# Two weight-block orders and two sign conventions for a seven-product block multiplication in a decoder layer

## The chip, the cores and the metric

The kernel runs on one core of a Trainium2 chip. The core has five engines with queues of their own: TensorE (PE in the profile; its weight loads are listed as PEld), VectorE (DVE), ScalarE (ACT), GpSimd (POOL) and SyncE (SP, which here only issues transfers). Each engine executes its queue in order and waits at semaphores for the others. The metric is the device time of one execution in microseconds (us); the median of three executions of the kernel before is 1702.04 us (1701.92 to 1702.26).

## What is computed

One decoder layer on 256 tokens of width 2048: a feed-forward block, a token mixer, a second feed-forward block, each with a residual sum, and a final norm.

```python
def swiglu(h, w_in, w_out):
    gu = h @ w_in                                # 2048 x 11264
    gate, up = gu[..., :D_FF], gu[..., D_FF:]
    return (jax.nn.silu(gate) * up) @ w_out      # 5632 x 2048

h = h + 0.5 * swiglu(rmsnorm(h, ffn1_norm[l]), ffn1_w_in[l], ffn1_w_out[l])
u = rmsnorm(h, mix_norm[l]) @ w_in_mix[l]
...
h = h + jnp.concatenate([y_pool, y_gla], axis=-1) @ w_out_mix[l]
h = h + 0.5 * swiglu(rmsnorm(h, ffn2_norm[l]), ffn2_w_in[l], ffn2_w_out[l])
return rmsnorm(h, final_norm)
```

All is float32. The change touches only the two `swiglu` blocks (and the way their weights are laid out), which take most of the time.

## The kernel before

**Precision.** A float32 product is made of three matmuls of a shorter type (`fp32r`): each operand is split into a high part (a rounding cast on ACT, line 155) and a low part (the source minus the high part, on DVE, line 156), and `three` (line 188) adds high x high, high x low and low x high. So each 128x512 block of weights costs ACT a cast and DVE a subtraction before PE can use it, and each product of a 128-token tile with a block costs PE three matmuls of 128x512.

**Steps.** Weights are streamed once, in steps of four blocks (1 MB): two 128-row blocks of the contraction by two 512-column blocks, B11 B12 / B21 B22. Activations of the same step are 2x2 blocks as well (two tiles of 128 tokens). There are two kinds of step:

- An S step (`s_step`, line 167, `Group.s`) is the plain 2x2 block product: 8 products, 24 matmuls. It splits the four blocks as they are: one 128x2048 subtraction on DVE where the buffers allow it.
- A W step (`w_step`, line 173, `Group.w`, line 260) is Winograd's form with 7 products, 21 matmuls. It needs sums of weight blocks (T1 to T4, made by `less`, line 179, on DVE, in place over the loaded blocks) and sums of activation blocks (S1 to S4, made once per pair of activation blocks by `s_factors`). It splits seven blocks: B11, B22, B21, then T1, T3, T2, T4. Three of the loaded blocks are therefore split before they are overwritten. Products shared between outputs are kept in two PSUM tiles of their own (`pw_...`), which `combine` (line 288) adds up when the last W step of a group is done (one ACT copy, four DVE operations of 128x512, then two of 128x1024 at line 483).

**Loops.** `ffn` (line 435) goes over 11 chunks of 512 gate and 512 up columns. `first_product(c)` takes 8 steps over the 2048 rows; which are W is given by `KINDS` (line 62): none in the first chunks, 4 or 5 of 8 in the next, then `CHUNKS`, 6 of 8 in each of the eight late chunks. The W steps come first in a chunk, over the activation pairs `W_PAIRS`; then the S steps. At the chunk's end come silu and product (lines 490 and 492), transposes on PE (line 499, output `ftp` or `ztp`) and a split (line 505). Between the chunks `second_product` takes S steps alone: 4 for each chunk. The output tiles on PE are named `ps_fi`, `pw_fi` (first product), `ps_fo` (second product) in the first feed-forward block and `ps_zi`, `pw_zi`, `ps_zo` in the second.

**Buffers.** Loaded steps go to a ring of raw buffers (`ring_raw`, 3, and one more per feed-forward block, `fring_raw` or `zring_raw`). Split blocks go to a ring of block buffers, high and low: 16 in `ring_hi`, `ring_lo`, and `MORE_RING` = 6 more in `fring_` or `zring_`, so 22. Blocks are taken in turn; a run of blocks that crosses the end of one part of the ring is split into two operations (`parts_of`, line 145). A block's buffer is free again when PE has done its last matmul with it.

**What sets the order.** The code is written step by step; the framework's scheduler, which uses a timeline model of its own, then sets each engine's queue, interleaving steps. The queues are fixed when the kernel is built.

Of the kernel before, what the change touches and what calls it, by code (L numbers as in the profile page):

```python
# [33 lines left out]
ALU = mybir.AluOpType  # L34
PSUM = bass.MemoryType.PSUM

P = 128
# [5 lines left out]
CW = 512  # L43
# [13 lines left out]
REACH = 16  # L57


W_PAIRS = (1, 3, 4, 6, 2, 5)  # L60
CHUNKS = ("WWWWWWSS",) * 8
KINDS = {
    "f": ("SSSSSSSS", "SSSSSSSS", "WWSWWWSS") + CHUNKS,
    "z": ("SSSSSSSS", "SWSWWWSS", "WWSWWWSS") + CHUNKS,
# [7 lines left out]
RAW_BUFS = 3  # L72
RING = 16
MORE_RAW = 1
MORE_RING = 6
WIDE = True
ROW_AT = 7
S_AT = 3
# [4 lines left out]
def layer(ctx: ExitStack, tc: tile.TileContext, io):  # L83
    nc = tc.nc
# [60 lines left out]
    def parts_of(src, runs, cw=CW):  # L145

        res = []
        for x in runs:
            i = x.start
            while i < x.stop:  # L150
                n, new = blocks.take(x.stop - i)
                hi, lo = (y[:, :, :cw] for y in new)
                for j in range(0, n, 2):
                    k = min(j + 2, n)
                    nc.scalar.copy(out=hi[:, j:k, :], in_=src[:, i + j : i + k, :])  # L155
                nc.vector.tensor_tensor(  # L156
                    out=lo, in0=src[:, i : i + n, :], in1=hi.bitcast(F32), op=ALU.subtract
                )
                res += [(hi[:, j, :], lo[:, j, :]) for j in range(n)]
                i += n  # L160
        return res

    ALL, PAIRS = (slice(0, 4),), (slice(0, 2), slice(2, 4))
# [3 lines left out]
    def s_step(src, parts=1, runs=WIDE):  # L167

        w = load(src, parts=max(parts, 2)).rearrange("p (b c) -> p b c", c=CW)
        b = parts_of(w, SINGLES if parts == 4 else PAIRS if parts == 2 or not WIDE else ALL)  # L170
        return lambda k, n: b[n if k == 0 else 3 - n]

    def w_step(src):

        w = load(src).rearrange("p (b c) -> p b c", c=CW)
        f = dict(zip(("B11", "B22", "B21"), parts_of(w, (slice(0, 1), slice(2, 4)))))

        def less(out, x, y):
            nc.vector.tensor_tensor(out=out, in0=x, in1=y, op=ALU.subtract)  # L179


        less(w[:, 0:2, :], w[:, 1:2, :].broadcast_to([P, 2, CW]), w[:, 0:4:2, :])
        less(w[:, 2, :], w[:, 2, :], w[:, 0, :])
        less(w[:, 3, :], w[:, 3, :], w[:, 2, :])
        f.update(zip(("T1", "T3", "T2", "T4"), parts_of(w, PAIRS)))
        return f

    def three(ps, a, b, start, stop, **kw):

        for i, (x, y) in enumerate(((a[0], b[0]), (a[0], b[1]), (a[1], b[0]))):  # L190
            nc.tensor.matmul(ps, x, y, start=start and i == 0, stop=stop and i == 2, **kw)  # L191

    class Group:
# [66 lines left out]
        def w(self, a, s, b):  # L260

            if self.one is None:
                self.one = [
                    self.psum[self.tags[1]].tile(
                        [P, 2, CW], F32, tag=self.tags[1], name=f"pw_{self.name}_{i}"
                    )
                    for i in range(2)
                ]
                first = True
            else:  # L270
                first = False
            self.left_w -= 1
            last = self.left_w == 0
            p16, p75 = self.one
            for (t, n), x, y in (((0, 0), a(0, 1), b["B21"]), ((0, 1), s["S4"], b["B22"])):
                ps, start, stop = self.target(t, n)
                three(ps, x, y, start, stop)
            three(p16[:, 0, :], a(0, 0), b["B11"], first, last)
            three(p75[:, 1, :], s["S1"], b["T1"], first, last)
            three(p75[:, 0, :], s["S3"], b["T3"], first, last)  # L280
            three(p16[:, 1, :], s["S2"], b["T2"], first, last)
            ps, start, stop = self.target(1, 0)
            three(ps, a(1, 1), b["T4"], start, stop)
            self.n += 1
            if last:
                self.combine()

        def combine(self):

            p16, p75 = self.one  # L290
            self.add = [
                ftmp[0].tile([P, 2, CW], F32, tag=f"add{t}", name=f"add_{self.name}_{t}")
                for t in range(NT)
            ]
            c, d = self.add
            u2 = d[:, 1, :]
            nc.scalar.copy(out=c[:, 0, :], in_=p16[:, 0, :])
            nc.vector.tensor_tensor(out=u2, in0=p16[:, 1, :], in1=c[:, 0, :], op=ALU.add)
            nc.vector.tensor_tensor(out=c[:, 1, :], in0=p75[:, 1, :], in1=u2, op=ALU.add)
            nc.vector.tensor_tensor(out=d[:, 0, :], in0=p75[:, 0, :], in1=u2, op=ALU.add)  # L300
            nc.vector.tensor_tensor(out=d[:, 1, :], in0=p75[:, 1, :], in1=d[:, 0, :], op=ALU.add)

# [345 lines left out]
    def finish1(np_, grp, h):  # L650
# [22 lines left out]
        finish1, first=x_ahead,  # L673
# [31 lines left out]
    for t in range(NT):  # L705
# [6 lines left out]
            out=gsil[t][:, gw[0] + gw[1] :], in_=ps[t][:, : gw[2]], func=AF.Silu, scale=rs(t)  # L712
# [13 lines left out]
    for t in range(NT):  # L726
        nc.vector.scalar_tensor_tensor(
            out=la[:, t, :], in0=z[t], scalar=0.0, in1=e[:, t, :], op0=ALU.min, op1=ALU.subtract
# [63 lines left out]
    for t in range(NT):  # L792
        sp = ps_t.tile([P, HEADS, P], F32, tag="tp", name=f"sp{t}")
        c = slice(t * P, (t + 1) * P)
# [339 lines left out]
```

## Time and profile before

| | |
|---|---|
| median of three executions | 1702.04 us |
| the profiled execution, span from first to last instruction | 1702.4 us |
| TensorE clock granted, mean | 0.998 |
| instructions on PE and on DVE in the profile | 7705 and 1565 |
| HBM read, written | 338.75 MB, 25.17 MB |
| stretches: first feed-forward block, mixer and its output product, second feed-forward block | about 0 to 700, 700 to 1000, 1000 to 1700 us |

In the profile a busy matmul overlaps the next one (matmuls are pipelined), so PE's busy share says little about how much of its rate is used; the distance between the starts of matmuls does. DVE's operations overlap at their ends too, by some 0.08 us. The span of the profiled execution stands 0.4 us above the median, so differences worked out in it can be taken from the median as they are.

### The profile page before, as it was taken

Reading aid. Unit: us, or ns where it says so; the run is one execution under the profiler, and the core shown is the slowest. Engines: PE = TensorE matmul, PEld = TensorE weight load, DVE = VectorE, ACT = ScalarE, POOL = GpSimd, SP = SyncE. Lnnn points to the kernel's source line nnn. Section 1 sums busy time; section 2 is a strip of 40 time slices with the busy share of each in tenths; the row PEclk is TensorE's granted clock in tenths of the full one; section 3 lists DMA queues with packets and bytes.
Section 4 is the critical chain, followed back from the end, with each engine's and each line's share of the span. In section 5 each row is a group of like instructions: output and inputs, shape, how many; then the busy total and the mean of one; then the engine's idle time right before and its main releaser. Section 6 shows DMA issues by size and latency. Waiting matters only on the chain.

```text
span 1702.4 us, 20984 instructions
## 1 busy us (share of the span) xinstructions
PE 1689.7 (99%) x7705; PEld 1403.1 (82%) x7705; DVE 1411.5 (83%) x1565; ACT 999.3 (59%) x1272; POOL 62.9 (4%) x70
## 2 busy tenths in 40 slices
PE   9999999999999999999999999999999999999997
PEld 7888888888888888888988888888888888888886
DVE  8779999999999996645564677999999999998974
ACT  7655666665666664563454554666656656566553
POOL 0000000000000000000000000000000000000012
PEclk9999999999999999999999999999999999999999
DMA  9856856857767776554665764676666667677781
GB/s 355 338 142 229 259 156 229 269 165 221 259 178 221 246 240 215 185 182 139 197 214 169 228 203 155 196 249 195 214 244 208 203 235 227 192 245 218 215 298 50
DMA packets 105241, 365.30 MB, mean 215 GB/s; under 512 B 11809, under 2 KB 15009, under 8 KB 105138
## 3 DMA queue, kind: packets, MB, share of 16 engines
q1 hardware_dynamic: 97026, 335.63, 58.1%
q0 software_dynamic: 7392, 27.27, 8.1%
q8 instruction: 60, 0.98, 0.2%
q10 hardware_dynamic: 720, 1.07, 0.2%
q14 instruction: 43, 0.35, 0.1%
HBM read 338.75 MB, written 25.17 MB: 214 GB/s over the span
## 4 chain that ended last, share of the span: by engine, by line
PE 91%; DVE 5%; DMA 2%; issue 1%; ACT 1%; SPq 0%; POOL 0%; POOLq 0%; ACTq 0%; DVEq 0%
PE ps_fi L191 17%; PE ps_zi L191 14%; PE ps_fo L191 14%; PE ps_zo L191 12%; PE pw_fi L191 8%; PE pw_zi L191 7%; PE ps_h L191 5%; PE ps_mp L191 3%; PE ps_mv L191 3%; DVE ring_lo L156 2%; PE ps_mg L191 2%; PE ps_mq L191 1%; DMA ring_raw<-in_ffn_w_out 1%; PE ps_w_mk L191 1%; DVE ring_raw L179 1%
## 5 line engine op out<-in xcount | busy, mean ns | idle before, releaser
L155 ACT CAST ring_hi<-ring_raw 128x1024 fp32r<-128x1024 f32 (+3 forms) x544 | 501.4, 942 | 381.6 <-DMA ring_raw<-in_ffn_w_in 79.8
L156 DVE TENSOR_TENSOR ring_lo<-ring_raw,ring_hi 128x1024 fp32r<-128x1024 f32 (+6 forms) x463 | 573.8, 1250 | 182.5 <-ACT ring_hi L155 181.4
L179 DVE TENSOR_TENSOR ring_raw<-ring_raw 128x512 f32<-128x512 f32 (+1 forms) x243 | 207.4, 862 | 0.3
L155 ACT CAST zring_hi<-ring_raw 128x1024 fp32r<-128x1024 f32 (+1 forms) x113 | 99.6, 887 | 54.5 <-DMA ring_raw<-in_ffn_w_out 11.8
L191 PE MATMUL ps_fi<-ring_lo,xT_hi 128*128 128x512 f32 x324 | 126.5, 390 | 0.5 <-DVE ring_lo L156 0.4
L191 PE MATMUL ps_fi<-ring_hi,xT_lo 128*128 128x512 f32 x324 | 125.8, 389 | 0.0
L191 PE MATMUL ps_fi<-ring_hi,xT_hi 128*128 128x512 f32 x324 | 124.2, 390 | 1.2 <-ACT ring_hi L155 1.2
L156 DVE TENSOR_TENSOR zring_lo<-ring_raw,zring_hi 128x1024 fp32r<-128x1024 f32 (+3 forms) x101 | 112.2, 1117 | 11.9 <-ACT zring_hi L155 11.8
L155 ACT CAST ring_hi<-zring_raw 128x1024 fp32r<-128x1024 f32 (+1 forms) x85 | 84.2, 991 | 48.0 <-PE ps_zi L191 22.8
L191 PE MATMUL ps_zi<-ring_lo,h_hi 128*128 128x512 f32 x288 | 112.1, 389 | 0.0
L191 PE MATMUL ps_zi<-ring_hi,h_lo 128*128 128x512 f32 x288 | 112.1, 390 | 0.0
L191 PE MATMUL ps_zi<-ring_hi,h_hi 128*128 128x512 f32 x288 | 111.3, 390 | 0.0
L156 DVE TENSOR_TENSOR ring_lo<-zring_raw,ring_hi 128x1024 fp32r<-128x1024 f32 (+2 forms) x65 | 94.2, 1451 | 7.4 <-ACT ring_hi L155 7.3
L191 PE MATMUL ps_fo<-ring_lo,fhi 128*128 128x512 f32 x240 | 93.9, 391 | 0.0
L191 PE MATMUL ps_fo<-ring_hi,flo 128*128 128x512 f32 x240 | 93.8, 391 | 0.0
L191 PE MATMUL ps_fo<-ring_hi,fhi 128*128 128x512 f32 x240 | 93.4, 391 | 0.0
L191 PE MATMUL pw_zi<-ring_hi,s_z 128*128 128x512 f32 x262 | 92.5, 389 | 0.0
L191 PE MATMUL ps_zo<-ring_lo,zhi 128*128 128x512 f32 x234 | 91.5, 391 | 0.0
L191 PE MATMUL ps_zo<-ring_hi,zlo 128*128 128x512 f32 x234 | 91.4, 391 | 0.0
L191 PE MATMUL ps_zo<-ring_hi,zhi 128*128 128x512 f32 x234 | 90.7, 390 | 0.0
L191 PE MATMUL pw_fi<-ring_hi,s_f 128*128 128x512 f32 x226 | 78.7, 389 | 0.0
L155 ACT CAST ring_hi<-fring_raw 128x512 fp32r<-128x512 f32 (+1 forms) x69 | 56.9, 832 | 33.6 <-DVE fring_raw L179 9.8
(324 smaller groups left out, 3730.5 us busy)
## 6 DMA issues: line engine op xcount, KB each, us to landing
ring_raw<-in_ffn_w_in SPq DMA_DIRECT2D x262, 512.0 KB, 5.6
ring_raw<-in_ffn_w_out SPq DMA_DIRECT2D x136, 512.0 KB, 5.2
fring_raw<-in_ffn_w_in SPq DMA_DIRECT2D x44, 512.0 KB, 5.5
zring_raw<-in_ffn_w_in SPq DMA_DIRECT2D x44, 512.0 KB, 4.3
ring_raw<-in_w_out_mix SPq DMA_DIRECT2D x32, 512.0 KB, 4.3
fring_raw<-in_ffn_w_out SPq DMA_DIRECT2D x20, 512.0 KB, 6.0
zring_raw<-in_ffn_w_out SPq DMA_DIRECT2D x20, 512.0 KB, 6.0
hd<-half_f POOLq DMA_DIRECT2D x18, 512.0 KB, 8.1
```

The costliest lines, as they stand in the source:

```text
L155: nc.scalar.copy(out=hi[:, j:k, :], in_=src[:, i + j : i + k, :])
L156: nc.vector.tensor_tensor(out=lo, in0=src[:, i : i + n, :], in1=hi.bitcast(F32), op=ALU.subtract)
L179: nc.vector.tensor_tensor(out=out, in0=x, in1=y, op=ALU.subtract)
L191: nc.tensor.matmul(ps, x, y, start=start and i == 0, stop=stop and i == 2, **kw)
```

## The change

It does five things.

1. The four blocks of a step are laid out B12, B11, B22, B21 in HBM instead of B11, B12, B22, B21 (`steps`, line 1083), and `s_step` picks them accordingly.
2. In `w_step` the three blocks that are needed as they are (B11, B22, B21) now lie side by side and are split in one call, and the four sums are split in another. The sums are made with other signs: Q1 = B11 + B12 in place of T1 = B12 - B11, with the whole second column of blocks turned in sign inside the form. There is an addition of 128x512 (line 181 of the kernel after), a subtraction of 128x512 and one of two blocks at once (line 179).
3. `combine` takes two differences instead of two sums.
4. `CHUNKS`: of the eight late chunks, the first, third, fifth and seventh have 7 W steps of 8; the others keep 6. Per feed-forward block that is four S steps that become W steps. `W_PAIRS` gets a seventh pair, 0, whose activation sums S1 to S4 have to be made and kept in each feed-forward block.
5. `MORE_RING` goes from 6 to 5: the block ring has 21 buffers.

```diff
--- before.py
+++ after.py
@@ -57,8 +57,8 @@
 REACH = 16
 
 
-W_PAIRS = (1, 3, 4, 6, 2, 5)
-CHUNKS = ("WWWWWWSS",) * 8
+W_PAIRS = (1, 3, 4, 6, 2, 5, 0)
+CHUNKS = ("WWWWWWWS", "WWWWWWSS") * 4
 KINDS = {
     "f": ("SSSSSSSS", "SSSSSSSS", "WWSWWWSS") + CHUNKS,
     "z": ("SSSSSSSS", "SWSWWWSS", "WWSWWWSS") + CHUNKS,
@@ -72,7 +72,7 @@
 RAW_BUFS = 3
 RING = 16
 MORE_RAW = 1
-MORE_RING = 6
+MORE_RING = 5
 WIDE = True
 ROW_AT = 7
 S_AT = 3
@@ -168,21 +168,20 @@
 
         w = load(src, parts=max(parts, 2)).rearrange("p (b c) -> p b c", c=CW)
         b = parts_of(w, SINGLES if parts == 4 else PAIRS if parts == 2 or not WIDE else ALL)
-        return lambda k, n: b[n if k == 0 else 3 - n]
+        return lambda k, n: b[1 - n if k == 0 else 3 - n]
 
     def w_step(src):
 
         w = load(src).rearrange("p (b c) -> p b c", c=CW)
-        f = dict(zip(("B11", "B22", "B21"), parts_of(w, (slice(0, 1), slice(2, 4)))))
+        f = dict(zip(("B11", "B22", "B21"), parts_of(w, (slice(1, 4),))))
 
         def less(out, x, y):
             nc.vector.tensor_tensor(out=out, in0=x, in1=y, op=ALU.subtract)
 
-
-        less(w[:, 0:2, :], w[:, 1:2, :].broadcast_to([P, 2, CW]), w[:, 0:4:2, :])
-        less(w[:, 2, :], w[:, 2, :], w[:, 0, :])
-        less(w[:, 3, :], w[:, 3, :], w[:, 2, :])
-        f.update(zip(("T1", "T3", "T2", "T4"), parts_of(w, PAIRS)))
+        nc.vector.tensor_tensor(out=w[:, 0, :], in0=w[:, 0, :], in1=w[:, 1, :], op=ALU.add)
+        less(w[:, 2, :], w[:, 0, :], w[:, 2, :])
+        less(w[:, 1:4:2, :], w[:, 1:4:2, :], w[:, 2:3, :].broadcast_to([P, 2, CW]))
+        f.update(zip(("Q1", "T3", "T2", "T4"), parts_of(w, ALL)))
         return f
 
     def three(ps, a, b, start, stop, **kw):
@@ -276,7 +275,7 @@
                 ps, start, stop = self.target(t, n)
                 three(ps, x, y, start, stop)
             three(p16[:, 0, :], a(0, 0), b["B11"], first, last)
-            three(p75[:, 1, :], s["S1"], b["T1"], first, last)
+            three(p75[:, 1, :], s["S1"], b["Q1"], first, last)
             three(p75[:, 0, :], s["S3"], b["T3"], first, last)
             three(p16[:, 1, :], s["S2"], b["T2"], first, last)
             ps, start, stop = self.target(1, 0)
@@ -296,9 +295,9 @@
             u2 = d[:, 1, :]
             nc.scalar.copy(out=c[:, 0, :], in_=p16[:, 0, :])
             nc.vector.tensor_tensor(out=u2, in0=p16[:, 1, :], in1=c[:, 0, :], op=ALU.add)
-            nc.vector.tensor_tensor(out=c[:, 1, :], in0=p75[:, 1, :], in1=u2, op=ALU.add)
+            nc.vector.tensor_tensor(out=c[:, 1, :], in0=p75[:, 1, :], in1=u2, op=ALU.subtract)
             nc.vector.tensor_tensor(out=d[:, 0, :], in0=p75[:, 0, :], in1=u2, op=ALU.add)
-            nc.vector.tensor_tensor(out=d[:, 1, :], in0=p75[:, 1, :], in1=d[:, 0, :], op=ALU.add)
+            nc.vector.tensor_tensor(out=d[:, 1, :], in0=p75[:, 1, :], in1=d[:, 0, :], op=ALU.subtract)
 
 
 
@@ -1080,7 +1079,7 @@
 
         b = np.stack([left, right], 2).reshape(-1, 2, P, left.shape[1], 2, CW)
         b = b.transpose(3, 0, 2, 1, 4, 5)
-        b = np.stack([b[:, :, :, 0, 0], b[:, :, :, 0, 1], b[:, :, :, 1, 1], b[:, :, :, 1, 0]], 3)
+        b = np.stack([b[:, :, :, 0, 1], b[:, :, :, 0, 0], b[:, :, :, 1, 1], b[:, :, :, 1, 0]], 3)
         return b.reshape(b.shape[0], b.shape[1], P, 4 * CW)
 
     def quads(w):
```

Built, the PE queue has 24 matmuls of 128x512 fewer (6942 in place of 6966), all from the eight changed steps; the DVE queue has 152 instructions fewer (1415 in place of 1567), and no transfer is added or taken away. Two places show how rows moved.

The first is the start of the program on PE, the first S step of the first chunk, whose four blocks are loaded and split one by one. `ps_fi_0` and `ps_fi_1` are the outputs of the two token tiles, `ring_hi` and `ring_lo` the parts of a weight block, `xT_hi` and `xT_lo` those of the activations; in brackets stands the engine whose semaphore is waited for. Before:

```order
L191 MATMUL ps_fi_0_137<-ring_hi,xT_hi_114 128x512 [waits Activation_49]
L191 MATMUL ps_fi_0_137<-ring_lo,xT_hi_114 128x512 [waits DVE_49]
L191 MATMUL ps_fi_0_137<-ring_hi,xT_lo_118 128x512
L191 MATMUL ps_fi_0_137<-ring_hi,xT_hi_114 128x512 [waits Activation_49]
L191 MATMUL ps_fi_0_137<-ring_lo,xT_hi_114 128x512 [waits DVE_49]
L191 MATMUL ps_fi_0_137<-ring_hi,xT_lo_118 128x512
L191 MATMUL ps_fi_0_137<-ring_hi,xT_hi_114 128x512 [waits Activation_49]
L191 MATMUL ps_fi_1_138<-ring_hi,xT_hi_114 128x512 [waits PE_49]
```

and after the change:

```order
L190 MATMUL ps_fi_0_137<-ring_hi,xT_hi_114 128x512 [waits Activation_49]
L190 MATMUL ps_fi_0_137<-ring_lo,xT_hi_114 128x512 [waits DVE_49]
L190 MATMUL ps_fi_0_137<-ring_hi,xT_lo_118 128x512
L190 MATMUL ps_fi_0_137<-ring_hi,xT_hi_114 128x512
L190 MATMUL ps_fi_0_137<-ring_lo,xT_hi_114 128x512
L190 MATMUL ps_fi_0_137<-ring_hi,xT_lo_118 128x512
L190 MATMUL ps_fi_0_137<-ring_hi,xT_hi_114 128x512 [waits Activation_49]
L190 MATMUL ps_fi_1_138<-ring_hi,xT_hi_114 128x512 [waits PE_49]
```

The first product now uses the second block to be loaded instead of the first, so the second product (fourth row) no longer waits for a cast; the seventh row, the first that uses the second row of blocks, waits for ACT in both.

The second place is DVE in the first feed-forward block, where the sums of the fourth chunk have been combined and the W steps of the fifth are being prepared. Rows with `fring_raw` as their source all belong to one W step; the others belong to the steps around it or to the chunk that has ended (`flo`). Before, from that step's first split to its last:

```order
L156 TENSOR_TENSOR ring_lo<-fring_raw,ring_hi 128x512
L156 TENSOR_TENSOR ring_lo<-fring_raw,ring_hi 128x1024
L179 TENSOR_TENSOR fring_raw<-fring_raw 128x1024
L179 TENSOR_TENSOR fring_raw<-fring_raw 128x512
L505 TENSOR_TENSOR flo_1587<-ftp_1577,fhi_1586 128x4x128
L179 TENSOR_TENSOR fring_raw<-fring_raw 128x512
L156 TENSOR_TENSOR ring_lo<-fring_raw,ring_hi 128x1024
L156 TENSOR_TENSOR fring_lo<-ring_raw,fring_hi 128x512
L156 TENSOR_TENSOR ring_lo<-fring_raw,ring_hi 128x512
L505 TENSOR_TENSOR flo_1587<-ftp_1577,fhi_1586 128x4x128
L156 TENSOR_TENSOR fring_lo<-fring_raw,fring_hi 128x512
```

and after the change, for the W step in the same place (its addition at line 181 stands some ten rows earlier, in between the chunk's sums):

```order
L156 TENSOR_TENSOR ring_lo<-fring_raw,ring_hi 128x1536
L179 TENSOR_TENSOR fring_raw<-fring_raw 128x512
L504 TENSOR_TENSOR flo_1579<-ftp_1569,fhi_1578 128x4x128
L181 TENSOR_TENSOR ring_raw<-ring_raw 128x512
L179 TENSOR_TENSOR fring_raw<-fring_raw 128x2x512
L156 TENSOR_TENSOR ring_lo<-ring_raw,ring_hi 128x1536
L504 TENSOR_TENSOR flo_1579<-ftp_1569,fhi_1578 128x4x128
L179 TENSOR_TENSOR ring_raw<-ring_raw 128x512
L156 TENSOR_TENSOR ring_lo<-fring_raw,ring_hi 128x2048
```

Eight operations have become five: the splits of one and two blocks are one of three blocks, the last three splits are one of four blocks (2048 columns), and the three operations on sums remain three. The last split, on which all four products with sums now wait, comes after the operation on two blocks and not before it in part.

## The prediction

> **What bounds the kernel now.** I read the page first, then PE's waits, then the distances between matmuls, then DVE by stretches. The page's busy times, two of its 40-slice rows and the chain that ended last:
>
> ```profile
> PE 1689.7 (99%) x7705; PEld 1403.1 (82%) x7705; DVE 1411.5 (83%) x1565; ACT 999.3 (59%) x1272; POOL 62.9 (4%) x70
> PE   9999999999999999999999999999999999999997
> DVE  8779999999999996645564677999999999998974
> ...
> PE 91%; DVE 5%; DMA 2%; issue 1%; ACT 1%; SPq 0%; POOL 0%; POOLq 0%; ACTq 0%; DVEq 0%
> ```
>
> PE is never idle, the chain runs over PE for 91%, but in both feed-forward blocks DVE has nines as well. So two engines are near their limits there. PE's own waits, all that the view of waits has for PE:
>
> ```profile
> PE idle L575 <- DVE zeros L570: 1.2, 1, 1.2
> PE ps_fi L191 <- ACT ring_hi L155: 1.2, 2, 0.8
> PE ps_fi L191 <- DVE ring_lo L156: 0.4, 2, 0.2
> ```
>
> That is under 3 us in 1702. Busy matmuls overlap, so I check that PE runs at its rate by their starts; this is the first and the last of 24 that follow each other in the second block (PE's timeline):
>
> ```profile
> 1195.66 0.39 PE L191 MATMUL ps_zi<-ring_hi,h_hi 128*128 128x512 f32 x1
> ...
> 1200.87 0.39 PE L191 MATMUL ps_zi<-ring_lo,h_hi 128*128 128x512 f32 x1
> ```
>
> 23 distances in 5.21 us are 0.2265 us each, which is what a matmul costs here (its "0.39" is mostly overlap). An S step's 24 take 5.44 us, a W step's 21 take 4.76 us. So PE, fed without a gap, sets the time, and a matmul taken away is worth 0.2265 us as long as DVE keeps feeding it. How near DVE is, over three late chunks of the second block (busy us and number of instructions by engine):
>
> ```profile
> 1161.00:1224.00 63.00, 63.00 (x284) 52.26 (x283) 58.60 (x61) 39.01 (x46) 2.23 (x3) 1.00 0.67 209
> 1224.00:1286.00 62.00, 62.00 (x279) 51.33 (x278) 59.44 (x62) 38.68 (x46) 1.71 (x2) 1.00 0.69 221
> 1286.00:1348.00 62.00, 62.00 (x279) 51.36 (x278) 57.75 (x61) 37.88 (x45) 1.71 (x2) 1.00 0.70 221
> sum 187.00, PE 187.00 PEld 154.95 DVE 175.79 ACT 115.57 POOL 5.66; mean PE 62.33 PEld 51.65 DVE 58.60 ACT 38.52 POOL 1.89
> ```
>
> DVE works 58.6 us of a chunk's 62.33, so 3.7 us are left. Where they lie decides much. The same view for a stretch in which DVE prepares W steps and one in which it prepares S steps:
>
> ```profile
> 1138.00:1184.00 46.00, 46.00 (x208) 38.08 (x207) 45.10 (x50) 28.03 (x34) 1.70 (x2) 1.00 0.61 177
> 1184.00:1196.00 12.00, 12.00 (x55) 9.94 (x54) 8.26 (x7) 7.55 (x9) 0.00 (x0) 1.00 0.95 331
> ```
>
> For W steps DVE is busy 98%; its rest is in the S steps (69%). There it waits for ACT, and ACT for buffers that PE still uses, or for a load:
>
> ```profile
> 1185.65 1.05 ACT L155 CAST ring_hi<-zring_raw 128x1024 fp32r<-128x1024 f32 x1 [3.47 <-PE ps_zi L191]
> ...
> 1191.60 1.05 ACT L155 CAST ring_hi<-ring_raw 128x1024 fp32r<-128x1024 f32 x1 [1.57 <-DMA ring_raw<-in_ffn_w_out]
> ```
>
> So this idle time is mostly DVE being ahead with a full ring: W steps use up a lead, S steps build it up again.
>
> **The change, part by part.**
>
> *Matmuls.* Eight S steps become W steps: 8 x 3 = 24 matmuls fewer, 24 x 0.2265 = **-5.4 us**, all on the path.
>
> *DVE's cost of a step.* What an operation costs is the distance to the next one that doesn't wait. Four rows without a wait between them:
>
> ```profile
> 1196.02 2.28 DVE L156 TENSOR_TENSOR ring_lo<-ring_raw,ring_hi 128x2048 fp32r<-128x2048 f32 x1
> 1198.22 0.68 DVE L298 TENSOR_TENSOR add_zi<-pw_zi,add_zi 128x512 f32<-128x512 f32 x1
> 1198.83 1.22 DVE L156 TENSOR_TENSOR zring_lo<-ring_raw,zring_hi 128x1024 fp32r<-128x1024 f32 x1
> 1199.96 0.68 DVE L299 TENSOR_TENSOR add_zi<-pw_zi,add_zi 128x512 f32<-128x512 f32 x1
> ```
>
> 512 columns cost 0.61, 1024 cost 1.13, 2048 cost 2.20; 1536 lie between, 1.67. A W step without cuts at the ring's ends is now 3 x 0.61 + 4 x 1.13 = 6.35 us and becomes 1.67 + 2 x 0.61 + 1.13 + 2.20 = 6.22; an S step stays at 2.20. Joining two operations saves only about 0.07 us. The Trainium skill (VectorE: DVE Perf Modes, The DRAIN you can't avoid) says that a next operation doesn't start before the pipe has emptied; then whole durations would count, a step's two operations fewer would be worth about 0.3 us, and the change would be nearly free for DVE. The starts above contradict it by 0.06 to 0.09 us an operation, so I keep the distances.
>
> A late chunk with 7 W steps: one more W step has 3.5 x 1024 more columns, each worth 2.20 - 1.13 = 1.07, so +3.75 us. 152 instructions fewer over 22 chunks are 7 a chunk, 7 x 0.07 = -0.5 us. DVE then needs 58.6 + 3.75 - 0.5 = 61.85 us, and PE 62.33 - 3 x 0.2265 = 61.65. A chunk with 6: 58.1 against 62.33. A pair: **119.95 of DVE in 123.98 of PE**. The spare shrinks from 7.5 to 4.0 us a pair, but stays positive, so on average DVE feeds PE.
>
> *The lead.* What counts is the worst moment, the end of a run of W steps. Four things shorten the lead there: the seventh W step uses up 6.22 - 4.76 = 1.46; the ring has one block fewer, a seventh of a W step, 0.68; all sums wait for one split of 2.20 where they waited for one of 1.13, 1.07; and DVE gains back 0.5. Together 2.7 us. How much is there now? A place where one value is written once and read once is the transpose at the chunk's end. The second `za` is written from 1145.74 on, and PE reads it at 1151.21:
>
> ```profile
> 1145.74 0.75 DVE L492 SCALAR_TENSOR_TENSOR za<-ps_zi,r_h_r,zs 128x512 f32<-128x512 f32 x1
> ...
> 1151.21 0.60 PE L499 MATMUL ztp<-ident,za 128*128 128x128 f32 x4
> ```
>
> The lead is 1151.21 - 1146.49 = 4.7 us, more than 2.7. But it isn't so everywhere. In the chain there is one place in the first block where the work goes from PE over DVE and a load back to PE:
>
> ```profile
> 438.96 2.21 DVE ring_lo L156
> 441.94 6.80 DMA ring_raw<-in_ffn_w_out
> 452.87 6.23 PE ps_fi L191 x26
> ```
>
> There no lead is left, and up to 2.7 us could become a wait; below nothing is excluded, since PE loses at most 0.4 us to `ring_lo` now. Between 0 and 2.7 I take 0.5, near the 0.4 that the row of waits shows: **+0.5 us**.
>
> *Activation sums of pair 0.* In each feed-forward block one addition of 512 columns, four of 128 and a split, besides a cast on ACT. Two rows of such work (an addition and two small ones):
>
> ```profile
> 10.43 0.69 DVE L410 TENSOR_TENSOR sa_f<-xT_hi,xT_lo 128x512 f32<-128x512 f32 x1
> 11.15 0.49 DVE L385 TENSOR_TENSOR sf_f<-sa_f 128x128 f32<-128x128 f32 x2
> ```
>
> That is 0.61 + 4 x 0.2 + 0.61 = 2.0 us of DVE in the first chunk, which has only S steps:
>
> ```profile
> 0.00:75.00 75.00, 72.33 (x308) 57.08 (x309) 60.37 (x86) 54.93 (x80) 3.79 (x11) 1.00 0.99 372
> 1000.00:1062.00 62.00, 62.00 (x283) 51.39 (x282) 49.90 (x80) 30.71 (x44) 2.76 (x2) 1.00 0.52 174
> ```
>
> DVE is idle for 14.6 and 12.1 us there, so **0**; without that cover 2.0 us each.
>
> *The start.* PE now begins with the second block. Rows of the start:
>
> ```profile
> 5.97 0.62 ACT L155 CAST ring_hi<-ring_raw 128x512 fp32r<-128x512 f32 x1 [0.41 <-DMA ring_raw<-in_ffn_w_in]
> 6.62 0.69 DVE L156 TENSOR_TENSOR ring_lo<-ring_raw,ring_hi 128x512 fp32r<-128x512 f32 x1 [0.34 <-ACT ring_hi L155]
> 7.60 1.27 ACT L155 CAST ring_hi<-ring_raw 128x512 fp32r<-128x512 f32 x2 [1.01 <-DMA ring_raw<-in_ffn_w_in]
> 8.93 0.73 PE L191 MATMUL ps_fi<-ring_hi,xT_hi 128*128 128x512 f32 x2 [0.82 <-ACT ring_hi L155]
> ```
>
> The second block's low part is there at 7.31. Five more matmuls end by about 8.5, before the seventh, which waits for the fourth cast until 8.93 as now. So **0**; were that wait gone, 1 us.
>
> *ACT and transfers.* Eight times three blocks more to cast are some 13 us over the whole, on an engine that is busy 38.5 of 62.33; transfers are the same. **0**.
>
> *Sum.* -5.4 + 0.5 = -4.9 on 1702.04: **1697.1 us**. The profiled span, 1702.4, lies 0.4 above the median, which changes no difference.
>
> **Rivals.** (1) *The lead is gone at the ends of the runs of seven.* PE then waits once in each of the eight such chunks. For it: the chunk needs more DVE time (61.85) than PE time (61.65), and one place has no lead already. Against it: 4.7 us at the transposes. At 0.25 to 1 us each this is 2 to 8 us: 1698.6 to 1704.6, about 1701, hardly distinct from no change.
>
> (2) *DVE becomes the bound.* Its idle time in the S steps need not be a full ring alone: with DMA busy 0.95 at 331 GB/s in that stretch and a wait of 1.57 us for a load, some of it is the wait for the next load, which would stay. If all 7.5 us a pair stayed, a pair would take 119.95 + 7.5 = 127.45 in place of 124.66: 8 x 2.8 = 22 us more, 1724 us. It decides from 124.66 - 119.95 = 4.7 us of idle time a pair that can't be given up; if 5.2 stay it is 4 us slower, 1706. Against it: for W steps DVE is busy 98% today, so it can run nearly without idle time when it is behind.
>
> (3) *The change doesn't do what it says*: the PE queue does hold 24 matmuls fewer, so this is out.
>
> **How the numbers follow.** The forecast has 0.57, rival 1 has 0.24, rival 2 has 0.16, and 0.03 are left for a time below 1696. A measurement of this kernel tells about 0.2% (3.4 us) from no change: the forecast (1696 to 1698.6) is faster, rival 1 the same, rival 2 slower. With 0.02 of the rest that makes 0.59 faster, 0.25 the same, 0.16 slower. The range takes the forecast and rival 1: 1695.8 to 1705.
>
> **What would show it.** Right: the distance of matmuls still 0.2265, PE's waits under 4 us, DVE at 96 to 98% in the late chunks, and less idle time in its S stretches. Rival 1: waits of PE for `ring_lo` of about 1 us at the ends of the odd late chunks. Rival 2: tens of such waits, late chunks of 63 us and more. The forecast is wrong if DVE's idle time per pair stays above 4 us while PE waits.

## The result, and the profile after

The changed kernel takes **1763.89 us** (median of four, 1762.51 to 1767.05) against 1701.98 us for the kernel before on the same chip: a ratio of 1.0362, 95% interval 1.0349 to 1.0376. It is 62 us slower; 5 us less had been predicted, and 1705 was the upper end of the range. The profiled execution spans 1763.2 us.

The page after: busy times, PE's and DVE's row of the 40 slices, the chain that ended last by engine.

```profile
PE 1708.7 (97%) x7681; PEld 1401.9 (80%) x7681; DVE 1435.5 (81%) x1413; ACT 1004.3 (57%) x1280; POOL 62.8 (4%) x70
...
PE   9999999999899999999999999999999999999997
...
DVE  8778898999899997655455676989899999999983
...
PE 17%; DVE 10%; DMA 5%; issue 3%; ACT 1%; POOL 0%; SPq 0%; POOLq 0%; DVEq 0%; ACTq 0%
```

PE has its 24 matmuls fewer. But the chain, which ran over PE for 91% before, now keeps changing engines; it could be followed for 36% of the span only, and PE has 17 of these 36. PE's own waits, the seven largest (engine, tile and line, what it waited for: us in all, times, longest):

```profile
PE pw_fi L190 <- DVE ring_lo L156: 8.9, 8, 2.2
PE pw_zi L190 <- DVE ring_lo L156: 7.1, 6, 2.1
PE pw_fi L190 <- ACT ring_hi L155: 5.5, 9, 1.6
PE ps_zo L190 <- DVE add_zi L297: 4.0, 2, 3.6
PE ps_fi L190 <- ACT ring_hi L155: 3.2, 5, 1.2
PE ps_zo L190 <- DVE ring_lo L156: 2.4, 1, 2.4
PE ps_zi L190 <- ACT ring_hi L155: 1.8, 1, 1.8
```

All that this view lists for PE adds up to 43.7 us in 46 waits; before it was 2.8 in 5. An idle time is counted from the modelled end of a matmul, 0.39 us after its start, although the next could have started after 0.2265; so each wait is worth some 0.16 us more than listed. Therefore I also took all distances between the starts of neighbouring 128x512 matmuls (without those of the first 21 us) and added up what each has over 0.2265 us. Distances over 0.26 us (waits above all) have 61.5 us of it after and 7.2 before: **+54.3**. A further kind, distances of 0.425 us, has 11.7 after and 2.4 before: **+9.3** (the last section has its place). With -5.4 for the matmuls that makes 58.2 of the 60.8 us that the span grew.

Is DVE the bound, then? Four pairs of late chunks of the second block, before, cut at the transposes (PE, PEld, DVE, ACT, POOL busy us and instructions):

```profile
1147.00:1274.00 127.00, 127.00 (x570) 105.24 (x569) 119.64 (x125) 78.08 (x91) 3.40 (x4) 1.00 0.68 216
...
sum 500.00, PE 499.92 PEld 413.24 DVE 470.28 ACT 309.32 POOL 22.17; mean PE 124.98 PEld 103.31 DVE 117.57 ACT 77.33 POOL 5.54
```

and after:

```profile
1197.00:1328.00 131.00, 125.39 (x543) 101.99 (x541) 120.30 (x106) 76.01 (x92) 2.56 (x3) 0.97 0.66 205
1328.00:1454.00 126.00, 123.69 (x548) 100.81 (x547) 121.09 (x107) 78.06 (x92) 3.47 (x4) 1.00 0.69 217
...
sum 512.00, PE 498.19 PEld 406.82 DVE 479.39 ACT 313.09 POOL 20.95; mean PE 124.55 PEld 101.70 DVE 119.85 ACT 78.27 POOL 5.24
```

DVE's work of a pair is 119.85 us, as predicted (119.95). But a pair now takes 128.0 us, and DVE is idle for 8.2 of them; before it was 125.0 and 7.4. Its idle time did not shrink when its work grew. The kernel is longer although DVE has room.

One such place, from the chain (start, duration, what):

```profile
1233.71 2.30 DVE ring_lo L156
...
1236.04 0.33 SPq L135
...
1236.45 7.13 DMA ring_raw<-in_ffn_w_out
...
1243.69 1.06 ACT ring_hi L155
...
1244.77 1.41 DVE ring_lo L156
...
1249.25 0.69 DVE add_zi L297
...
1249.99 2.43 PE ps_zo L190 x5
```

and DVE's queue there:

```profile
1241.00 1.22 DVE L156 TENSOR_TENSOR zring_lo<-ring_raw,zring_hi 128x1024 fp32r<-128x1024 f32 x1
1244.77 2.29 DVE L156 TENSOR_TENSOR ring_lo<-ring_raw,ring_hi 128x2048 fp32r<-128x2048 f32 x1 [2.55 <-ACT ring_hi L155]
1246.98 0.68 DVE L181 TENSOR_TENSOR ring_raw<-ring_raw 128x512 f32<-128x512 f32 x1
1247.58 1.75 DVE L156 TENSOR_TENSOR ring_lo<-zring_raw,ring_hi 128x1536 fp32r<-128x1536 f32 x1
1249.25 0.68 DVE L297 TENSOR_TENSOR add_zi<-pw_zi,add_zi 128x512 f32<-128x512 f32 x1
```

Read it backwards. PE waits 3.6 us for the addition of `combine`. That stands in DVE's queue behind three operations; the first of them waits 2.55 us for a cast, the cast for a load that lasted 7.13 us, and the load for a raw buffer that DVE released only at 1236.02, with a split. (The median of such loads, from issue to landing, is 4.9 to 6.4 us in this profile.) So the loop is: DVE releases a raw buffer, the load follows, ACT casts, DVE splits; and as DVE's queue has a fixed order, whatever stands behind the split waits with it.

Where the 60.8 us arise, by the start of the transposes that end a chunk (PE's timeline):

| up to the end of | before | after | later by |
|---|---|---|---|
| first block, chunk 1 | 99.3 | 100.1 | 0.8 |
| first block, chunk 2 | 157.8 | 162.7 | 4.9 |
| first block, chunk 9 | 595.3 | 628.9 | 33.6 |
| second block, chunk 0 | 1049.3 | 1082.6 | 33.3 |
| second block, chunk 2 | 1147.3 | 1196.8 | 49.5 |
| second block, chunk 10 | 1646.8 | 1709.3 | 62.5 |

The late chunks are 3 to 10. So 16.2 us come from chunks 1 and 2 of the second block, whose W steps did not become more: the seventh W step cannot be all.

### The profile page after: what moved, and what is told of

The parts are those of the page before. It is cut to its first block, busy times and chain, and to the rows that moved or that the text cites. A ratio compares the mean times of both kernels' runs of the same rounds, so it can differ in the third digit from the quotient of the medians.

```text
span 1763.2 us, 20702 instructions
## 1 busy us (share of the span) xinstructions
PE 1708.7 (97%) x7681; PEld 1401.9 (80%) x7681; DVE 1435.5 (81%) x1413; ACT 1004.3 (57%) x1280; POOL 62.8 (4%) x70
## 5 line engine op out<-in xcount | busy, mean ns | idle before, releaser
L156 DVE TENSOR_TENSOR ring_lo<-ring_raw,ring_hi 128x2048 fp32r<-128x2048 f32 (+7 forms) x381 | 593.9, 1569 | 190.3 <-ACT ring_hi L155 189.0
L155 ACT CAST ring_hi<-ring_raw 128x1024 fp32r<-128x1024 f32 (+3 forms) x583 | 527.5, 934 | 371.8 <-DVE ring_raw L179 58.3
L179 DVE TENSOR_TENSOR ring_raw<-ring_raw 128x512 f32<-128x512 f32 (+1 forms) x178 | 168.0, 952 | 0.4
L190 PE MATMUL ps_fo<-ring_hi,fhi 128*128 128x512 f32 x286 | 111.8, 392 | 1.7 <-DVE add_fi L297 1.7
L190 PE MATMUL ps_zo<-ring_hi,zhi 128*128 128x512 f32 x278 | 109.3, 394 | 4.0 <-DVE add_zi L297 4.0
L155 ACT CAST zring_hi<-ring_raw 128x1024 fp32r<-128x1024 f32 (+1 forms) x80 | 69.5, 883 | 60.9 <-PE pw_zi L190 24.3
L155 ACT CAST ring_hi<-fring_raw 128x1024 fp32r<-128x1024 f32 (+1 forms) x80 | 74.9, 958 | 42.1 <-DMA fring_raw<-in_ffn_w_in 17.3
L156 DVE TENSOR_TENSOR zring_lo<-ring_raw,zring_hi 128x1536 fp32r<-128x1536 f32 (+3 forms) x55 | 77.0, 1403 | 15.9 <-ACT zring_hi L155 15.8
L156 DVE TENSOR_TENSOR ring_lo<-fring_raw,ring_hi 128x2048 fp32r<-128x2048 f32 (+3 forms) x45 | 83.1, 1847 | 6.6 <-ACT ring_hi L155 6.4
L155 ACT CAST fring_hi<-ring_raw 128x1024 fp32r<-128x1024 f32 (+1 forms) x73 | 65.0, 904 | 39.3 <-DVE ring_raw L179 13.4
```

What stands on the lines that cost most here:

```text
L156: nc.vector.tensor_tensor(out=lo, in0=src[:, i : i + n, :], in1=hi.bitcast(F32), op=ALU.subtract)
```

## The experiments

Every kernel below is built anew, so the scheduler may give its queues another order; the price of an edit contains that, and no run holds the order fixed. Times are medians, ratios are against the kernel before on the same chip, with 95% intervals. "16+5" is `RING` + `MORE_RING`, the late ring blocks; "raw" is the number of raw buffers in the feed-forward blocks.

| kernel | form | late W steps | raw | blocks | us | ratio |
|---|---|---|---|---|---|---|
| before | old | 6 | 4 | 16+6 | 1702 to 1703 | 1 |
| after | new | 7/6 | 4 | 16+5 | 1763.9 | 1.0362 (1.0349 to 1.0376) |
| form6_r22 | new | 6 | 4 | 16+6 | 1762.4 | 1.0349 (1.0334 to 1.0365) |
| form6_r21 | new | 6 | 4 | 16+5 | 1745.4 | 1.0240 (1.0221 to 1.0259) |
| old7_r21 | old | 7/6 | 4 | 16+5 | 1767.4 | 1.0384 (1.0355 to 1.0412) |
| old6_r21 | old | 6 | 4 | 16+5 | 1753.5 | 1.0304 (1.0279 to 1.0330) |
| old6_r20 | old | 6 | 4 | 16+4 | 1715.3 | 1.0069 (1.0053 to 1.0086) |
| old6_raw5_r20 | old | 6 | 5 | 16+4 | 1704.2 | 1.0007 (0.9997 to 1.0017) |
| old6_r22_15_7 | old | 6 | 4 | 15+7 | 1703.3 | 0.9998 (0.9989 to 1.0007) |
| new7_r21_two | new, sums split two and two | 7/6 | 4 | 16+5 | 1766.2 | 1.0361 (1.0335 to 1.0387) |
| new7_raw5_r19 | new | 7/6 | 5 | 16+3 | 1793.3 | 1.0540 (1.0511 to 1.0569) |
| form6_raw5_r20 | new | 6 | 5 | 16+4 | 1742.1 | 1.0234 (1.0219 to 1.0250) |
| old7_raw5_r19 | old | 7/6 | 5 | 16+3 | 1737.1 | 1.0205 (1.0188 to 1.0222) |
| new7_r20 | new | 7/6 | 4 | 16+4 | 1800.4 | 1.0595 (1.0556 to 1.0633) |
| form6_15_7_narrow | new signs, old grain | 6 | 4 | 15+7 | 1719.0 | 1.0092 (1.0077 to 1.0107) |
| form6_15_7_sums2 | new, sums split two and two | 6 | 4 | 15+7 | 1752.7 | 1.0296 (1.0272 to 1.0320) |
| form6_15_7_blocks2 | new, loaded blocks one and two | 6 | 4 | 15+7 | 1736.0 | 1.0192 (1.0171 to 1.0213) |
| form6_15_7_wide | new | 6 | 4 | 15+7 | 1756.4 | 1.0308 (1.0290 to 1.0325) |
| form6_14_7_narrow | new signs, old grain | 6 | 4 | 14+7 | 1711.5 | 1.0054 (1.0039 to 1.0069) |
| form7_14_7_narrow | new signs, old grain | 7/6 | 4 | 14+7 | 1763.3 | 1.0362 (1.0331 to 1.0393) |

### One part of the change at a time

```diff
 form6_r22, form6_r21: the changed kernel with
-W_PAIRS = (1, 3, 4, 6, 2, 5, 0)
-CHUNKS = ("WWWWWWWS", "WWWWWWSS") * 4
+W_PAIRS = (1, 3, 4, 6, 2, 5)
+CHUNKS = ("WWWWWWSS",) * 8
 and in form6_r22 MORE_RING = 6
 old7_r21: the kernel before with the changed kernel's W_PAIRS, CHUNKS, MORE_RING
 old6_r21: the kernel before with MORE_RING = 5
```

> The new block order, signs and wide splits alone: 6 W steps in every late chunk, 22 blocks in the ring, as before. PE has the same number of matmuls as before. If the wide splits (all four sums wait for one split of 2048 columns) are what starves PE, this takes most of the 62 us too: 1735 to 1760. If the seventh W step is the cause, it is within 5 us of 1702. If the three parts only add up to it together, 1705 to 1720.

> As the run before, with 21 blocks in the ring, so the kernel after without the seventh W step and its sums. If the seventh W step is the cause, within 5 us of 1702. If the ring's size is, clearly slower than with 22 blocks, by 10 us and more. If the wide splits are, 1735 to 1760 as with 22 blocks.

> The old form and block order with the new mix of steps: 7 W steps in every second late chunk, seven activation pairs, 21 blocks. 24 matmuls fewer than before, as after. If the seventh W step is the cause, 1750 or more, since the old form needs slightly more of DVE. If the wide splits are, near 1697 to 1705.

> The kernel before with 21 blocks in the ring and nothing else changed. If one block of lead (0.7 us of PE) were decisive, 1720 or more; if not, within 4 us of 1702.

Each part alone brings most of the loss: the form 60 us, the seventh step with its smaller ring 65, the smaller ring by itself 51. They do not add up, so they are not independent; that they meet in one thing which each of them uses up is a guess. And a smaller ring is not always bad: in the new form 21 blocks are 17 us faster than 22 (1745.4 against 1762.4).

### Is it the lead in the ring, the load loop, or one wide split?

```diff
 old6_r20, old6_raw5_r20, old6_r22_15_7: the kernel before with
-MORE_RING = 6
+MORE_RING = 4                    # old6_r20
+MORE_RING = 4, MORE_RAW = 2      # old6_raw5_r20
+MORE_RING = 7, RING = 15         # old6_r22_15_7
 new7_r21_two: the changed kernel with
-        f.update(zip(("Q1", "T3", "T2", "T4"), parts_of(w, ALL)))
+        f.update(zip(("Q1", "T3", "T2", "T4"), parts_of(w, PAIRS)))
```

> The kernel before with 20 ring blocks in place of 22, nothing else changed (21 blocks gave 1753.5). If what counts is how far the queues can run ahead (every block less is a lead lost), 20 blocks are worse than 21: 1765 to 1800. If what counts is how the order of the work and the cuts at the ring's end happen to fall together, 20 blocks (which are cut at other places) may come out on either side of 1753, and below it, 1715 to 1745, excludes the lead alone.

> The kernel before with 20 ring blocks and one more buffer for loaded weights in the feed-forward blocks (about the same memory). If the loop that binds the disturbed kernels is a raw buffer released by DVE, loaded anew in 6 to 7 us, cast and split, one more such buffer takes the loop off the path although the ring is smaller: 1702 to 1712, and waits of ACT and DVE for loads fall to well under the 165 us of the kernel before. If the ring's lead or the order alone counts, it stays at 1745 or more.

> The kernel before with its 22 late ring blocks as 15+7 in place of 16+6, so that only the early stages have one block fewer. If 22 blocks (a chunk of six W steps takes 66, three turns of the ring) are what keeps the late chunks free of waits: 1700 to 1708. If any departure from the order of before brings the waits on: 1735 or more.

> The changed kernel (1763.9) with its four sums split by two calls of two blocks in place of one of four; matmuls, sums and buffers as in the changed kernel. If the one wide split, for which all sums wait and which holds the loaded buffer longer, is the main cause: 1735 to 1750. If any seventh W step or the smaller ring brings the waits, whatever the split: 1755 to 1775.

20 blocks are far better than 21 (1715.3 against 1753.5), so the loss with a smaller ring is not a lead that shrinks block by block. A fifth raw buffer brings the old form with 20 blocks back to the time of before. What it takes away, from the view of ACT's waits, without it and with it:

```profile
ACT ring_hi L155 <- DMA ring_raw<-in_ffn_w_in: 53.0, 39, 4.2
```

```profile
ACT ring_hi L155 <- DMA ring_raw<-in_ffn_w_in: 5.2, 9, 1.5
```

All of ACT's waits for loads fall from 138 to 62 us. The size of these waits doesn't measure the loss, for the kernel before has 165 us of them and is not slow; what speaks for the loop over the raw buffers is that the fifth buffer takes away 11 of the 12 us. That holds for 20 blocks; at 21 blocks, where the old form loses 51 us, the fifth buffer was not tried. For the changed kernel, undoing the one wide split of the sums alone does nothing: 1766.2.

### The same cure on the new form and on the seventh step

```diff
 new7_raw5_r19, new7_r20: the changed kernel; form6_raw5_r20: form6_r21; old7_raw5_r19: old7_r21, with
-MORE_RAW = 1
-MORE_RING = 5
+MORE_RAW = 2, MORE_RING = 3      # new7_raw5_r19, old7_raw5_r19
+MORE_RAW = 2, MORE_RING = 4      # form6_raw5_r20
+MORE_RING = 4                    # new7_r20
```

> The changed kernel (1763.9) with one more buffer for loaded weights and 19 late ring blocks in place of 21. If the loop of release, load, cast and split is what costs the changed kernel its 62 us, as it did in the kernel before with 20 blocks (1715 without and 1704 with the buffer), most of it goes: 1700 to 1715, PE's waits under 10 us. If the new form's order or a ring that is too small for its four sums at once is the cause, it stays at 1740 or more.

> The new form with six W steps in every late chunk (1762.4 with 22 blocks and 1745.4 with 21, four loaded buffers), now with five loaded buffers and 20 blocks. Loop over loaded buffers as the cause: 1700 to 1712. The form itself (its wide split, its holding of blocks) as the cause: 1735 or more.

> The old form with seven W steps in every second late chunk (1767.4 with 21 blocks and four loaded buffers), now with five loaded buffers and 19 blocks. Loop as the cause: 1697 to 1712, and near 1697 if the 24 matmuls fewer are then worth their 5.4 us. DVE's extra work of the seventh step (about 123.7 us of DVE in 124 us a pair of chunks) or the order as the cause: 1735 or more.

> The changed kernel with 20 late ring blocks in place of 21 and nothing else changed. The old form went from 1753 at 21 blocks to 1715 at 20. If 21 blocks are bad for what they cut, in both forms, this is clearly below 1764: 1720 to 1745. If the new form waits for its loads whatever the ring: 1755 or more.

My theory of the raw loop alone falls here: with the fifth buffer the new form stays at 1742 (1745 without), the changed kernel goes to 1793, and the old form with seven W steps comes down by 30 us, to 1737, and no further. The test is not clean, since each of these kernels also gave up one or two ring blocks for the buffer; against the changed kernel with 20 blocks and four buffers, the one with 19 and five is 7 us faster. The number of blocks has no simple direction either: 20 in place of 21 made the old form faster and the changed kernel 36 us slower.

### The grain of the splits

Four kernels with the new signs, six W steps and 22 blocks differ in the grain alone.

```diff
 form6_15_7_wide: form6_r22 with RING = 15, MORE_RING = 7; in the others
-        f = dict(zip(("B11", "B22", "B21"), parts_of(w, (slice(1, 4),))))
+        f = dict(zip(("B11", "B22", "B21"), parts_of(w, (slice(1, 2), slice(2, 4)))))   # narrow, blocks2
...
-        f.update(zip(("Q1", "T3", "T2", "T4"), parts_of(w, ALL)))
+        f.update(zip(("Q1", "T3", "T2", "T4"), parts_of(w, PAIRS)))                      # narrow, sums2
```

> New layout and signs, six W steps in every late chunk, 22 late ring blocks cut 15+7 (the old form at this size: 1703.3), but the splits as narrow as in the kernel before: B11 alone, B22 and B21 together, the sums two and two. If it is the widening of the splits that costs: 1702 to 1712. If it is the new signs themselves (three sums that follow each other before all but one of the four can be split, the loaded first half held 4 us longer): 1730 or more.

> As the narrow one, but the three loaded blocks split in one operation; the sums still two and two. If the widening costs, this has one of its two parts: 1712 to 1730. If the widening of the sums alone costs: as the narrow one, within 4 us. If the signs cost: 1730 or more, as the narrow one.

> As the narrow one, but the four sums split in one operation; the loaded blocks one and two. If the widening costs, this has the larger of its two parts: 1720 to 1745. If only the three loaded blocks' widening costs: as the narrow one.

> Both splits wide, as in the changed kernel, with six W steps and 22 blocks cut 15+7 (cut 16+6 it took 1762.4). If the widening costs: 1735 to 1765, most of the 62 us of the changed kernel without a seventh W step. If the cut at the ring's end made the 1762.4: 1710 or less.

Against 1703.3 of the old form with these buffers: signs and layout **+15.7** (narrow), the three loaded blocks in one operation **+33.7** on top, the sums in one **+17.0**, both **+37.4**. The narrow kernel lies between the numbers of the two theories, so the signs seem to have a price of their own; the split of the loaded blocks, which I had held for the smaller part, is the larger one. These are prices in this ring, of one build each: with one block fewer the narrow kernel takes 1711.5 (next section), 7 us less, so the smaller prices may be the ring's or the order's.

What the wide split of the loaded blocks does, from the view of ACT's waits (whole execution), with narrow splits

```profile
ACT ring_hi L155 <- DMA ring_raw<-in_ffn_w_in: 78.2, 46, 6.1
...
ACT ring_hi L155 <- DVE ring_raw L179: 55.8, 42, 6.2
```

and with the three loaded blocks in one (sums2):

```profile
ACT ring_hi L155 <- DVE ring_raw L179: 87.7, 41, 5.4
ACT ring_hi L155 <- DMA ring_raw<-in_ffn_w_in: 85.6, 52, 5.3
```

ACT waits 32 us more for DVE's sums (L179) and 7 us more for loads. DVE in turn waits more for ACT, from its view of waits, narrow first:

```profile
DVE ring_lo L156 <- ACT ring_hi L155: 175.9, 123, 10.0
```

```profile
DVE ring_lo L156 <- ACT ring_hi L155: 206.3, 140, 7.6
```

A wide split can begin only when all three blocks, so both halves of the load, are cast; the sums overwrite those blocks and come behind it, and the next casts behind the sums. But ACT's wait for the sums can't be the price of wide splits in general: with both splits wide the row of 87.7 is 34.9, and that kernel is the slowest of the four. What is larger in every wider kernel is the part of DVE's idle time that ends with a load, either directly or through a cast that had itself waited for one (counted in the trace; where the cast had not waited, the last one before it that had). It is 61 us in the old form with these buffers, 81 in the narrow kernel, 90 with the sums in one, 130 with the loaded blocks in one and 123 with both, at 1703.3, 1719.0, 1736.0, 1752.7 and 1756.4 us. That the later start of a wide split is what makes these loads late is argued, not shown.

### The seventh W step by itself

```diff
 form6_14_7_narrow: form6_15_7_narrow with RING = 14
 form7_14_7_narrow: the same with the changed kernel's
+W_PAIRS = (1, 3, 4, 6, 2, 5, 0)
+CHUNKS = ("WWWWWWWS", "WWWWWWSS") * 4
```

> Narrow splits, new signs, six W steps, 21 late ring blocks cut 14+7: the base for the next kernel. One block fewer than the narrow kernel with 22 (1719.0). If 21 blocks are bad as such (the old form took 1753.5 with 16+5): 1750 or more. If the cut decides: 1715 to 1735.

> The same with seven W steps in every second late chunk, nothing else changed. If DVE's spare time of 7.5 us a pair of chunks is there to be used, as the prediction had it, the 24 matmuls fewer show: 5 us below the kernel with six. If the spare time is what covers the waits for loads and casts, PE waits in its place: 20 to 45 us above the kernel with six. Old form, 21 blocks cut 16+5: 14 us above.

+51.8 us for 24 matmuls fewer, more than either expectation had; the base, 1711.5, lies below what was expected of it too. In the other two pairs of kernels that differ in this step alone (each time with the sums of pair 0) it costs 13.8 us (old form, 16+5 blocks, 1753.5 to 1767.4) and 18.5 (new form, 16+5, 1745.4 to 1763.9). So it is a loss in all three, of a size that hangs on form and ring. Four pairs of late chunks of the second block, six W steps and then seven (last row of the view of stretches):

```profile
sum 497.00, PE 493.99 PEld 406.78 DVE 468.08 ACT 307.68 POOL 20.24; mean PE 123.50 PEld 101.69 DVE 117.02 ACT 76.92 POOL 5.06
```

```profile
sum 518.00, PE 502.46 PEld 406.86 DVE 482.97 ACT 312.28 POOL 24.74; mean PE 125.62 PEld 101.72 DVE 120.74 ACT 78.07 POOL 6.18
```

DVE's work grows by 120.74 - 117.02 = 3.7 us a pair. The pair grows from 124.25 to 129.5, so DVE's idle time is 7.2 and then 8.8 us. Two rows of DVE's waits over the whole execution, six and then seven W steps:

```profile
DVE ring_lo L156 <- ACT ring_hi L155: 176.8, 128, 5.8
...
DVE ring_raw L181 <- DMA ring_raw<-in_ffn_w_in: 15.0, 14, 3.5
```

```profile
DVE ring_lo L156 <- ACT ring_hi L155: 176.4, 124, 5.8
DVE ring_raw L181 <- DMA ring_raw<-in_ffn_w_in: 30.8, 22, 4.6
```

The wait for casts is the same to 0.4 us, the direct wait for loads doubles; but most of the first row lies outside these four pairs. Within them, counted as above, 26.7 of DVE's 28.8 us of idle time end with a load, and with seven W steps 28.8 of 34.8. So in these chunks it was hardly a reserve. By the page, the chain runs over PE for 67% with six and for

```profile
PE 44%; DVE 32%; DMA 16%; issue 5%; ACT 2%; SPq 0%; POOL 0%; DVEq 0%; POOLq 0%; ACTq 0%
```

with seven.

## Why the prediction was wrong, step by step

- **Matmuls, -5.4:** right as far as it goes. PE has 24 fewer, and where it is fed the distance is still 0.2265 us; "as long as DVE keeps feeding it" was the condition that failed.
- **DVE's cost of a step:** right. 1536 columns were taken as 1.67; in the queue above, the split that starts at 1247.58 is followed at 1249.25, 1.67 later, and the addition before it takes 0.60. Whole durations, 1.75 and 0.68, don't count there. The section of the Trainium skill that the prediction set against its distances (VectorE: DVE Perf Modes, The DRAIN you can't avoid) says itself that a next operation that is not held, that is, not made to wait for all earlier ones, starts earlier; this trace agrees, by 0.08 us. A pair's 119.95 came out as 119.85; of that the growth is 2.3, where 2.75 had been added up.
- **"The spare shrinks from 7.5 to 4.0 us a pair, but stays positive, so on average DVE feeds PE":** this step failed. It takes DVE's idle time for a lead that can be given up ("mostly DVE being ahead with a full ring"), on the strength of the 98% in W stretches and of one wait of ACT for PE. The trace of the kernel before says otherwise, when each idle time of DVE in the four late pairs is followed to what the cast that ended it had waited for: of 29.5 us, 20.4 end with a load and 9.0 with PE, which is the most that a full ring can account for. It shows already at the two casts in the prediction's fence; DVE's own waits for them were the other way round, the longer one behind the cast that had waited for a load (DVE's timeline, before):

```profile
1186.74 2.29 DVE L156 TENSOR_TENSOR ring_lo<-zring_raw,ring_hi 128x2048 fp32r<-128x2048 f32 x1 [1.23 <-ACT ring_hi L155]
...
1192.68 1.22 DVE L156 TENSOR_TENSOR ring_lo<-ring_raw,ring_hi 128x1024 fp32r<-128x1024 f32 x1 [2.51 <-ACT ring_hi L155]
```

  So 5.1 us a pair were waits for loads from the start, more than the 4.7 that decide rival 2; after the change it is 21.7 of 31.7 us, 5.4 a pair. DVE's idle time per pair went from 7.4 to 8.2, and with the seventh step alone from 7.2 to 8.8. Rival 2 had this mechanism and its point of decision (4.7 us that can't be given up) and a chance of 0.16. Its size was short too: 22 us for the eight pairs. In the second block it fits: four pairs took 512 in place of 500 us, 12 more, where it had 11. But the late chunks of the first block lost 28.7 up to chunk 9 alone, where it had 11 for all of them, and for chunks 1 and 2 of the second, which lost 16.2, it had no term. The last sentence of the forecast, that it is wrong if DVE's idle time per pair stays above 4 us while PE waits, is what happened.
- **The lead, 2.7 of 4.7 us, +0.5:** failed in the same way. One block fewer was worth 0.68 us there; by itself (old6_r21) it costs 51 us, and two fewer cost 12. The 4.7 us were read at one transpose; what gives way lies elsewhere, with 20 blocks in the raw loop, with 21 it is open.
- **Joined operations, -0.07 us each:** the sum counted what DVE saves and not what must be ready before a wide operation can start. The grain costs 37 us with six W steps and 15+7 blocks, the signs 16 there and 9 with 14+7 (1711.5 against the kernel before). For the signs, the trace shows a change in the raw buffers. Before, SP's queue (the loads) was released in two ways, by DVE's splits and by the sums at L179:

```profile
SPq L135 <- DVE ring_lo L156: 1007.7, 348, 11.8
...
SPq L135 <- DVE ring_raw L179: 91.3, 23, 9.3
```

  After, the second row is gone, and the first is

```profile
SPq L135 <- DVE ring_lo L156: 1134.5, 314, 15.1
```

  In the old form the first difference makes two sums of the first loaded half at once, which then comes free early. In the new one all but Q1 hang on each other (Q1, then T2, then T3 and T4), and the half stays until the last split. From the start of its first reader to the end of its last, the first half of a W step is held 11.0 us before and 23.6 after (means of 110 and 118 halves), 10.8 and 22.4 with 15+7 blocks in the old form and the narrow new one. Part of this is an earlier first reader: before, it is a cast, on average 10.5 us after the load has landed; after, it is in 98 of the 118 the addition of Q1 on DVE, and the mean is 1.4 us. So a load that is late now stops DVE itself: its direct waits for loads are 28.5 us after and none before. But the narrow kernel with 14+7 blocks has these figures too (22.3 us, 0.9 us) and loses 9 us, so by themselves they cost no more than that. That this is the whole price of the signs was not tried.
- **S sums of pair 0, the start, 0:** the first block is 0.8 us behind at the end of chunk 1, so at most that.
- **ACT and transfers, 0:** transfers are the same, and ACT's busy time rose by 5 us, where 13 had been reckoned. But ACT's place in the loop counts: what DVE waits for most is ACT, and ACT waits for loads and for DVE's sums.

Settled is that DVE's idle time was not there to be used, and that each of two things costs much without the other: the seventh W step (+51.8 with narrow splits and 14+7 blocks, 14 to 18 with 16+5) and the new form with its wide splits (+53.1 with six W steps and 15+7 blocks). In the changed kernel they cost 62 us together, hardly more than one of them at its dearest; that both use up the same slack is argued. How the 62 us divide between them, the ring and the order of the queues is open. Open also is why a given ring is good or bad: 16+5 costs the old form 51 us and 16+4 only 12, and the narrow new form is better with 14+7 (1711.5) than with 15+7 (1719.0). The cuts at the ring's end and the queues' order change together there, and how much of the order changes doesn't tell: of the 7646 matmuls of PE's queue, 5663 write the same output tile as at the same place of the kernel before with 15+7 blocks (as fast) and 5687 with 16+5 (51 us slower). No kernel tried beats the one before; 15+7 blocks and the fifth raw buffer equal it within 0.2%.

## What to carry to other kernels

An engine's idle time is a reserve only if it ends with a full buffer, so follow each idle time to what its releaser had waited for; if that is a load or the work of another engine, it stays when work is added, and the engine beside it pays. In a loop of load, cast, split and release, price an edit by when its inputs are all there and when its buffers come free, not by its own duration: a wider operation can be later on both counts. And if a kernel with queues fixed at build time waits nowhere, build it with one buffer more and one less before trusting a gain of 0.3%: here the same work came out anywhere from 1702 to 1754 us.

## What the hardware showed that I had not expected

After a wait PE can run at half its rate for a while. PE's timeline at the place shown above (start, duration, operation, idle time before it):

```profile
1249.99 0.73 PE L190 MATMUL ps_zo<-ring_hi,zhi 128*128 128x512 f32 x1 [3.64 <-DVE add_zi L297]
1250.51 0.63 PE L190 MATMUL ps_zo<-ring_lo,zhi 128*128 128x512 f32 x1
1250.94 0.63 PE L190 MATMUL ps_zo<-ring_hi,zlo 128*128 128x512 f32 x1
...
1253.50 0.41 PE L190 MATMUL ps_zo<-ring_hi,zlo 128*128 128x512 f32 x1
1253.74 0.40 PE L190 MATMUL ps_zo<-ring_hi,zhi 128*128 128x512 f32 x1
```

From 1250.51 the distance is 0.427 us for seven matmuls, then 0.23 again; the clock granted from 1250.5 to 1253.5 is 0.50, and over that pair of chunks 0.97. The changed kernel has seven such stretches of six to eight matmuls, some 0.2 us lost on each, about 10 us in all; the longest idle time of PE that is listed just before each was 1.1 to 3.6 us, and in six of them under 2.2. Eight other idle times of 1.1 us and more after the start, the longest of 2.4, were followed by none, so it is not the length of the wait alone; and the kernel before has one such stretch, at 748.65 us in the mixer, with no idle time listed just before it but small matmuls (17 partitions) among the large. The Trainium skill (TensorE: Matmul & The Clock Gate, HAM oscillation — how this bites in real kernels) puts the rule as no idle gaps of PE over about 3.4 us; here six of the seven came behind shorter gaps. So a wait's price can be more than its length, by up to 1.6 us.
